# Attention's matmuls in an order written out: projections in steps of twelve, and between them one step of GLA, softmax heads or norms

## The chip, the cores and the metric

The kernel runs on one core of a Trainium2 chip (trn2). The metric is device time in microseconds (us) of one execution. TensorE (PE) multiplies, VectorE (DVE) and ScalarE (ACT) work on tiles and empty PSUM banks, GpSimd (POOL) does a little of that and issues some transfers, SyncE (SP) issues the other transfers. Each engine takes its own instructions strictly in their order.

## The reference

One decoder layer over 512 tokens of width 2048:

```python
xn = rms_norm(h, attn_norm_g)
(gq, gk, gv, gg, ga, fq, fk, fv, fg, ff, mq, mg) = split(xn @ w_in)
log_a = log_sigmoid(ga @ gla_a_w2 + gla_a_b) / 16
gla_o = gla_chunked(heads(gq), heads(gk), heads(gv), heads(log_a))        # 8 heads, dk 64, dv 128
fox_o = forgetting_attention(rms_norm(fq), rms_norm(fk), fv, log_sigmoid(ff + fox_f_b))  # 4 heads of 128, causal
mk, mv = split(rms_norm(mem) @ w_mem_kv)                                  # 256 memory tokens
mem_o = softmax(rms_norm(mq) @ rms_norm(mk).T * 128 ** -0.5) @ mv         # 4 heads of 128
o = rms_norm(concat(gla_o, fox_o, mem_o)) per head
h = x + (o * [silu(gg) | sigmoid(fg) | sigmoid(mg)]) @ w_out
y = h + relu(rms_norm(h, mlp_norm_g) @ w_up) ** 2 @ w_down                # d_ff 8192
```

GLA is a gated linear recurrence: a state per head, decayed by the gates and updated by k^T v. FoX is softmax attention with a cumulative forget term added to the logits.

## The kernel before, in words

All large products are done in three matmuls each: both operands are split into a high part (a cast to a shorter float, on ACT) and a low part (the difference, on DVE), and `mm3` (lines 152 to 156) adds high x high, high x low and low x high. `wtile` (line 136) loads a weight tile through SP's queue and makes both parts; `Weights.split` (line 352) does the same for the blocked products. The stages, in the order of the program:

1. `gk` and `gq` are projected (`project`, line 431), 16 tiles of 128 input columns each.
2. The pairs gv0/gv1 and fq/fk are computed by `in_pair` (line 491) and `multiply` (line 374), with seven block products in place of eight. `ORDER` gives their sequence 1, 5, 6, 3, 7, 2, 4. Four of the seven left operands are sums of blocks of x. `x_sums` (line 447) makes them: the eight tiles of x are read again, ACT multiplies in the gain, POOL makes four sums per tile pair (`block_sums`, line 275, with the engine G), ACT and DVE split them into `sh` and `sl`. This is done before the pairs for the first half of the input columns, and after product 7 of the second pair for the second half. Some differences of weight blocks (`Pair.minus`, line 480) run on POOL too.
3. The constants of attention (masks `tri16`, `suf16`, `cmask`, `lmask`) are made on POOL, lines 523 to 557, in buffers that the pair stage frees.
4. Attention. The 48 columns of gates are projected ("small", line 566). GLA (lines 630 to 742) runs over four chunks of 128 tokens. In each chunk seven levels of block sizes 128 to 2 fill the score matrix: a level takes two differences, an exponential, two products with q into `ql`, one with k, a matmul into `lp`, and a masked copy into `sc`. Then the outputs (line 719) add the state's part (line 715, whose operands have 64 rows) and the state is renewed. Softmax heads go through `attend` (line 402), one head at a time: logits, row maximum, exponential, transposes, product with v. `normed_T` (line 226) and `turned_heads` (line 790) normalise heads and transpose them. Between these stand the projections `fv`, `mq`, the memory's k and v, and the four gates `gg0`, `gg1`, `fg`, `mg`.
5. After each gate projection lines 898 to 918 form the gated heads and the seven left operands of the output product; some go through DRAM (`out_op`).
6. The output product (`out_pair`, line 974), then eight blocks of up and eight of down.

The order of instructions on each engine is set by a planner. It takes them in the order of the program as a priority, moved forward by `high_priority(offset)`, and places what it expects to be ready. `AHEAD` is 3000, `GLA_AHEAD` is 300, `urgent` is 2 x AHEAD. Two pools of four PSUM banks each exist: `gbank` for projections and `abank` for everything else. In the output product the residual block x is loaded by `block` (line 977, priority 300) and added to the product's bank by DVE in `after` (line 988); product 6 goes on in the bank of product 1, so it waits for that addition. Left operands that went through DRAM are read back by `fetch` and split by `resplit` (lines 1051 to 1055, code lines 857 to 868).

Of the kernel before, what the change touches and what calls it, by code (L numbers as in the profile page):

```python
# [15 lines left out]
S = 512  # L16
# [30 lines left out]
def hybrid_layer(  # L47
# [58 lines left out]
    one_c = wide[:, S - 1 : S]  # L106
    fbt = const.tile([FH, 1], F32, name="fbt")
# [5 lines left out]
    def rsqrt(dst, ss, n, inv, name):  # L113

        s, y, z = (const.tile([128, n], F32, name=f"{v}_{name}", tag=f"rs_{v}{n}", bufs=2) for v in "syz")
# [93 lines left out]
    def head_rms(src, nh, name, hd=128):  # L209

        sq = tmp(f"sq_{name}", "tb", nh * hd)
        A.activation(sq, src, AF.Square)
        ss = tp.tile([128, nh], F32, tag="hss", name=f"hss_{name}")
        V.tensor_reduce(ss, sq.rearrange("p (h d) -> p h d", h=nh), AX.X, ALU.add)
        r = tp.tile([128, nh], F32, tag="hr", name=f"hr_{name}", bufs=4)
        rsqrt(r, ss, nh, 1.0 / hd, name)
        return r

    def scaled(dst, ps, rstd, t):
        with tc.high_priority(offset=AHEAD):  # L220
            if t % 2 == 0:
                A.activation(dst, ps, AF.Copy, scale=rstd)  # L222
            else:
                V.tensor_scalar(dst, ps, rstd, None, op0=ALU.mult)

    def normed_T(raw, gain, scale, dst, name):

        r = head_rms(raw, 4, name)
        nrm = tmp(f"nrm_{name}", "tc")
        V.tensor_mul(  # L230
            nrm.rearrange("p (h d) -> p h d", h=4),
            raw.rearrange("p (h d) -> p h d", h=4),
            r.unsqueeze(2).broadcast_to([128, 4, 128]),
        )
        tps = abank(f"tps_{name}")
        for h in range(4):
            T.transpose(tps[:, h * 128 : h * 128 + 128], nrm[:, h * 128 : h * 128 + 128], ident)
        V.tensor_scalar(
            dst, tps.rearrange("p (h t) -> p h t", h=4), gain, scale, op0=ALU.mult, op1=ALU.mult
        )  # L240


    def project(*groups, turned=False, first=False, bank=gbank, order=range(NK // 2)):

        first_k, last_k = 2 * order[0], 2 * order[-1] + 1
        banks = [[(abank if i else bank)(f"{g}_{t}") for t in range(NT)] for i, g in enumerate(groups)]
        for kp in order:
            for ps, group in zip(banks, groups):
                wh, wl = wtile(w_in[GROUPS.index(group), kp], f"{group}{kp}", parts=2 if first and not kp else 1)
                for kk in range(2):  # L250
                    k = 2 * kp + kk
                    ah, al = x_tile(k)
                    for t in range(NT):
                        if turned:
                            cs = slice(kk * 512 + t * 128, kk * 512 + t * 128 + 128)
                            mm3(ps[t], wh[:, cs], wl[:, cs], ah, al, k == first_k, k == last_k)
                        else:
                            cs = slice(kk * 512, kk * 512 + 512)
                            sl = slice(t * 128, t * 128 + 128)
                            mm3(ps[t], ah[:, sl], al[:, sl], wh[:, cs], wl[:, cs], k == first_k, k == last_k)  # L260
        return [p for ps in banks for p in ps]
# [112 lines left out]
    def multiply(w, after, inside=None):  # L374
# [27 lines left out]
    def attend(n, logits, rowmax, v, dst, name):  # L402

        av = abank(f"av_{name}")
# [852 lines left out]
```

## Time and profile before

| what | value |
|---|---|
| median of 3 runs | 2187.0 us (2181.78 to 2187.2) |
| the profiled execution's own time | 2185.21 us |
| its span, first to last instruction | 2183.5 us |
| PE busy | 2126.2 us, 97% |
| DVE busy | 1631.3 us, 75% |
| ACT busy | 1123.2 us, 51% |
| POOL busy | 213.0 us, 10% |
| mean granted clock | 0.993 |

A row of a timeline gives the start in us from the span's start, the length, the engine, the line, the operation, output <- inputs, and the count; the square bracket at the end gives the engine's idle time before it and what ended it. A row of instruction groups gives after the bar the busy time, the mean length of one in ns, and the idle time before. Lengths of matmuls overlap, so the spacing of their starts is the measure of throughput. A short matmul on 32-bit floats is counted as two instructions.

### The profile page before, as it was taken

To read this page: it belongs to the slowest core of one execution; us is meant where nothing else is said; L and a number is where in the kernel's file an instruction comes from. 1 tells how busy PE (TensorE), PEld (TensorE's weight loads), DVE (VectorE), ACT (ScalarE), POOL (GpSimd) and SP (SyncE) were. 2 spreads that over 40 slices of the span, in tenths; PEclk is the share of its full clock that TensorE was granted. 3 is DMA by queue.
4 is the path that set the end of the run, shared out by engine and by line. 5 is a ranking of instruction groups with operands and counts; after the bars stand their busy time and mean duration, and the time that the engine had idled before them with its cause. 6 is when DMAs were issued, how large, how long until landed. Compare 5 with 4: busy or idle time off the path is not lost.

```text
span 2183.5 us, 25488 instructions
## 1 busy us (share of the span) xinstructions
PE 2126.2 (97%) x9746; PEld 1728.5 (79%) x9746; DVE 1631.3 (75%) x1800; ACT 1123.2 (51%) x1535; POOL 213.0 (10%) x245
## 2 busy tenths in 40 slices
PE   8999999989999889999999999999999999999999
PEld 7887777767777668878888888888788788788787
DVE  6579977884666779887768768769868767877875
ACT  6454433344564545755554555556646545556443
POOL 1346100000000003100000000000000000000000
PEclk9999999999999989999999999999999999999999
DMA  7333211241213455533543443455577678668654
GB/s 269 102 118 112 87 59 49 88 143 39 88 61 132 180 217 212 211 117 141 177 144 137 167 168 120 162 182 193 195 219 203 183 202 248 168 191 253 182 167 131
DMA packets 74628, 339.24 MB, mean 155 GB/s; under 512 B 8633, under 2 KB 10681, under 8 KB 53002
## 3 DMA queue, kind: packets, MB, share of 16 engines
q1 hardware_dynamic: 55898, 270.76, 35.3%
q0 software_dynamic: 18608, 66.86, 11.7%
q8 instruction: 76, 1.25, 0.2%
q14 instruction: 46, 0.38, 0.1%
HBM read 266.54 MB, written 71.04 MB: 155 GB/s over the span
## 4 chain that ended last, share of the span: by engine, by line
PE 78%; DVE 11%; DMA 4%; issue 3%; ACT 2%; POOL 1%; SPq 0%; DVEq 0%; ACTq 0%; POOLq 0%
PE acc_up L154 9%; PE acc_up L155 9%; PE acc_up L156 9%; PE acc_dn L155 7%; PE acc_dn L156 7%; PE acc_dn L154 7%; PE acc_out L154 2%; PE acc_out L155 2%; PE acc_out L156 2%; DMA left1l<-op 2%; DVE hl_dn L370 1%; DVE raw_dn L332 1%; DMA left5l<-op 1%; PE gg L154 1%; PE ut L1072 1%
## 5 line engine op out<-in xcount | busy, mean ns | idle before, releaser
L370 DVE TENSOR_TENSOR hl_up<-raw_up,hl_up 128x1024 fp32r<-128x1024 f32 x224 | 271.6, 1221 | 141.6 <-ACT hl_up L370 141.5
L370 ACT CAST hl_up<-raw_up 128x1024 fp32r<-128x1024 f32 x224 | 235.3, 1052 | 253.7 <-PE acc_up L156 193.9
L370 DVE TENSOR_TENSOR hl_dn<-raw_dn,hl_dn 128x1024 fp32r<-128x1024 f32 x224 | 270.5, 1221 | 99.5 <-ACT hl_dn L370 98.7
L370 ACT CAST hl_dn<-raw_dn 128x1024 fp32r<-128x1024 f32 x224 | 234.4, 1053 | 204.6 <-PE acc_dn L156 163.5
L332 DVE TENSOR_TENSOR raw_dn<-raw_dn,raw_dn 128x2048 f32<-128x2048 f32 x64 | 146.1, 2286 | 16.1 <-DMA raw_dn<-in_w_down_dram 15.9
L332 DVE TENSOR_TENSOR raw_up<-raw_up,raw_up 128x2048 f32<-128x2048 f32 x64 | 145.1, 2267 | 1.4 <-DMA raw_up<-in_w_up_dram 1.3
L370 ACT CAST hl_out<-raw_out 128x1024 fp32r<-128x1024 f32 x56 | 58.7, 1052 | 68.6 <-PE acc_out L156 55.3
L1172 POOL DMA_DIRECT2D hd<-m x48 | 41.0, 854 | 516.1 <-ACT m L1171 516.1
L370 DVE TENSOR_TENSOR hl_out<-raw_out,hl_out 128x1024 fp32r<-128x1024 f32 x56 | 69.2, 1253 | 25.0 <-ACT hl_out L370 25.0
L1171 ACT COPY m<-acc_dn 128x512 f32<-128x512 f32 x96 | 54.5, 587 | 30.3 <-PE acc_dn L156 30.3
L1064 POOL DMA_DIRECT2D op<-u x32 | 17.1, 534 | 486.3 <-ACT u L1073 479.1
L370 DVE TENSOR_TENSOR hl_hl_in<-spare,hl_hl_in 128x1024 fp32r<-128x1024 f32 x31 | 45.6, 1481 | 15.6 <-ACT hl_hl_in L370 15.6
L154 PE MATMUL gg<-ahi_x,hl_gg 128*128 128x512 f32 x128 | 54.6, 427 | 2.6 <-ACT raw_mk L222 2.2
L370 ACT CAST hl_hl_in<-spare 128x1024 fp32r<-128x1024 f32 x31 | 32.5, 1049 | 43.4 <-PE acc_in L156 18.9
L155 PE MATMUL acc_dn<-hl_dn,left 128*128 128x512 f32 x128 | 50.3, 393 | 4.6 <-DVE hl_dn L370 4.6
L155 PE MATMUL gg<-alo_x,hl_gg 128*128 128x512 f32 x128 | 53.7, 419 | 0.0
L156 PE MATMUL gg<-ahi_x,hl_gg 128*128 128x512 f32 x128 | 53.2, 415 | 0.0
L154 PE MATMUL acc_up<-hl_up,left 128*128 128x512 f32 x128 | 49.9, 390 | 3.1 <-ACT z L1127 3.1
L155 PE MATMUL acc_in<-hl_hl_in,sh 128*128 128x512 f32 x128 | 50.2, 392 | 2.6 <-DVE hl_hl_in L370 2.6
L155 PE MATMUL acc_dn<-hl_dn,left0h 128*128 128x512 f32 x128 | 50.2, 392 | 1.2 <-DVE hl_dn L370 1.2
L154 PE MATMUL acc_in<-hl_hl_in,sh 128*128 128x512 f32 x128 | 49.9, 390 | 0.7 <-DVE o L499 0.7
L155 PE MATMUL acc_dn<-hl_dn,left3h 128*128 128x512 f32 x128 | 50.5, 395 | 0.0
(566 smaller groups left out, 6320.0 us busy)
## 6 DMA issues: line engine op xcount, KB each, us to landing
raw_up<-in_w_up_dram SPq DMA_DIRECT2D x64, 1024.0 KB, 4.8
raw_dn<-in_w_down_dram SPq DMA_DIRECT2D x64, 1024.0 KB, 6.8
hd<-m POOLq DMA_DIRECT2D x48, 512.0 KB, 5.6
raw_out<-in_w_out_dram SPq DMA_DIRECT2D x16, 1024.0 KB, 5.7
op<-u POOLq DMA_DIRECT2D x32, 512.0 KB, 3.8
op<-s POOLq DMA_DIRECT2D x24, 512.0 KB, 2.9
spare<-in_w_pair_dram SPq DMA_DIRECT2D x16, 512.0 KB, 4.3
raw_in<-in_w_pair_dram SPq DMA_DIRECT2D x16, 512.0 KB, 3.6
```

What stands on the lines that cost most here:

```text
L154: T.matmul(ps, lhsT=ah, rhs=bh, start=start, stop=False, skip_group_check=on)
L155: T.matmul(ps, lhsT=ah, rhs=bl, start=False, stop=False, skip_group_check=on)
L156: T.matmul(ps, lhsT=al, rhs=bh, start=False, stop=stop, skip_group_check=on)
L332: V.tensor_sub(dst, a, b)
L370: made = A.copy(hi, part), V.tensor_sub(lo, part, hi.bitcast(F32))
L1064: nc.gpsimd.dma_start(down_op[c][i][:, half * 1024 : half * 1024 + 1024], tile)
L1072: T.transpose(tps[:, m * 128 : m * 128 + 128], z[:, t * 512 + m * 128 : t * 512 + m * 128 + 128], ident)
L1171: A.copy(st[:, t * 512 : t * 512 + 512], acc[t])
L1172: nc.gpsimd.dma_start(dst, st.rearrange("p (t n) -> p t n", t=2), accum_op=ALU.add)
```

## The change

- **Order.** Attention is rewritten as a generator, `steps`, that runs beside another, `projections`. `projections` hands over after every 12 matmuls (one input tile of a projection). Each `yield n` of attention asks for n such steps before its next burst. Afterwards all PE instructions from "small" to the end of `mg` are chained one behind the other as they were traced, so the planner no longer chooses among them.
- **GLA.** Levels are prepared in pairs one step ahead; the product with k covers only the first half of each block; the state's part uses `qz`, a zero-padded copy of q with 128 rows per head.
- **Softmax.** Heads with short rows share a bank (one, two or four heads), and a three-stage pipeline (`one`: logits, maximum, exponential; `two`: transposes; `three`: product with v) moves one bank per step.
- **Norms.** Sums of squares come from ACT's accumulation, 128 columns at a time, and two blocks share one reciprocal root; transposed results are written by ACT instead of DVE.
- **Operands of the output product.** `place` gives them their buffers only after the memory heads; what the first three gates made by then goes through DRAM and is read back there.
- **Sums of x.** DVE makes them. Those of the second half are made before the pairs, written to DRAM (`x_op`), and read back by operand after products 5, 6, 3 and 7 of the second pair.
- **Output product.** The last gate's banks come from `gbank`, so products 1 and 5 of the first output block swap pools; the x blocks of the first half are loaded with priority 3 x AHEAD.

```diff
             first = p in (1, 5, 2)
             if q == 0 and first:
-                chain[p] = [(gbank if p == 1 else abank)(f"acc_{w.name}_{p}_{i}") for i in range(2)]
+                chain[p] = [(gbank if p == (5 if w.name == "out0" else 1) else abank)(f"acc_{w.name}_{p}_{i}") for i in range(2)]
             acc = chain[p if first else 5 if p == 3 else 1]
...
-    sh = [bp.tile([128, 2, 4, 256], FR, name=f"sh{i}") for i in range(2)]
+    sh = bp.tile([128, 4, 4, 256], FR, name="sh")
...
+    x_op = [dram.tile([128, 4, 256], F32, name=f"x_op{i}") for i in range(4)]
...
-            for _ in block_sums(a1[:, :256], a2[:, :256], a1[:, 256:], a2[:, 256:], temps.get, G):
+            for _ in block_sums(a1[:, :256], a2[:, :256], a1[:, 256:], a2[:, 256:], temps.get):
                 pass
             for i in range(2):
-                hi, lo = (w[j // 2][:, j % 2, 2 * i : 2 * i + 2, :] for w in (sh, sl))
                 src = st[i].rearrange("p (s t) -> p s t", s=2)
-                A.copy(hi, src)
-                V.tensor_sub(lo, src, hi.bitcast(F32))
+                if c:
+                    for s in range(2):
+                        nc.gpsimd.dma_start(x_op[2 * i + s][:, j, :], src[:, s, :])
+                else:
+                    hi, lo = sh[:, 2 * i : 2 * i + 2, j, :], sl[i][:, :, j, :]
+                    A.copy(hi, src)
+                    V.tensor_sub(lo, src, hi.bitcast(F32))
+
+    def next_sums(n):
+        hi, lo = sh[:, n, :, :], sl[n // 2][:, n % 2, :, :]
+        nc.sync.dma_start(lo.bitcast(F32), x_op[n])
+        A.copy(hi, lo.bitcast(F32))
+        V.tensor_sub(lo, lo.bitcast(F32), hi.bitcast(F32))
...
-            if (c, n, p) == (0, 1, 7):
+            if (c, n) == (0, 1) and p in SUMS:
                 with tc.high_priority(offset=AHEAD):
-                    x_sums(1)
+                    next_sums(SUMS[p])
...
     with tc.high_priority(offset=400):
         x_sums(0)
+    x_sums(1)
     for c in range(2):
...
+    def head_rms(srcs, name):
+
+        ss = tp.tile([128, 8], F32, tag="hss", name=f"hss_{name}")
+        for i, src in enumerate(srcs):
+            sq = tmp(f"sq_{name}{i}", "tb")
+            for h in range(4):
+                cs = slice(h * 128, h * 128 + 128)
+                A.activation(sq[:, cs], src[:, cs], AF.Square, accum_out=ss[:, 4 * i + h : 4 * i + h + 1])
+        r = tp.tile([128, 8], F32, tag="hr", name=f"hr_{name}", bufs=4)
+        rsqrt(r, ss, 8, 1.0 / 128, name)
+        return r
...
+    def norms(srcs, gain, dsts, name, wait):
+
+        for a in range(0, len(srcs), 2):
+            r = head_rms(srcs[a : a + 2], f"{name}{a}")
+            nrm = [tmp(f"nrm_{name}{a + i}", "tc") for i in range(2)]
+            for i in range(2):
+                normed(nrm[i], srcs[a + i], r[:, 4 * i : 4 * i + 4])
+            yield wait
+            for i in range(2):
+                tps = abank(f"tps_{name}{a + i}")
+                for h in range(4):
+                    T.transpose(tps[:, h * 128 : h * 128 + 128], nrm[i][:, h * 128 : h * 128 + 128], ident)
+                A.activation(dsts[a + i], tps.rearrange("p (h t) -> p h t", h=4), AF.Copy, scale=gain)
...
+        V.tensor_sub(ev[:, :, :hb], ref, bv[:, :, :hb])
+        V.tensor_sub(ev[:, :, hb:], bv[:, :, hb:], ref)
+        A.activation(e, e, AF.Exp)
+        ql = qls[li % 2]
+        for s in range(2):
+            rows = slice(s * 64, s * 64 + 64)
+            V.tensor_mul(
+                ql[rows, :, s, :].rearrange("p h (n b) -> p h n b", b=hb),
+                qTs[rows, c, :].rearrange("p (h n b) -> p h n b", h=4, b=B)[:, :, :, hb:],
+                e[rows, :].rearrange("p (h n b) -> p h n b", h=4, b=B)[:, :, :, hb:],
+            )
+
+        V.tensor_mul(ev[:, :, :hb], ev[:, :, :hb], blocks_of(kTs[:, c, :], B)[:, :, :hb])
+        return li, e, ql
...
+    def gla(g):
+        state = tmp("state", "rbx")
+        bT, eb, kd = decays(0, g)
         for c in range(NT):
-            if c == 2:
-                for t in range(NT):
-                    normed_T(o[:, t, 1536:2048], g_fk, 1.0, fkT[:, :, t * 128 : t * 128 + 128], f"fk{t}")
-            qT, kT = qTs[:, c, :], kTs[:, c, :]
-
...
+
+            qk = tmp(f"qk_{c}", "tc")
+            G.tensor_tensor(qk, qTs[:, c, :], kTs[:, c, :], op=ALU.mult)
+            ready = [level(c, li, bT) for li in (0, 1)]
+            yield 2 if c else 3
+            for a in (0, 2, 4, 6):
+                lps = [(li, level_scores(c, li, e, ql)) for li, e, ql in ready]
+                if a == 4 and c < NT - 1:
+                    g = decay_logs(c + 1)
+                if a == 6:
+                    dps = abank(f"dg_{c}")
+                    for p in range(4):
+                        T.matmul(
+                            dps[:, 2 * p : 2 * p + 2], lhsT=qk[:, p * 128 : p * 128 + 128], rhs=sel,
+                            start=True, stop=True,
+                        )
+                    dg = tp.tile([128, GH], F32, tag="dg", name=f"dg_{c}")
+                    V.tensor_copy(dg, dps[:, :GH])
+                for li, lp in lps:
+                    place_scores(li, lp)
+                ready = [level(c, li, bT) for li in (a + 2, a + 3) if li < len(LEVELS)]
+                if a == 4 and c:
+                    for s in range(2):
+                        rows = slice(s * 64, s * 64 + 64)
+                        V.tensor_mul(qz[rows, :, s, :], heads4(qTs[:, c, :])[rows], heads4(eb)[rows])
+                yield 3 if a in (0, 4) else 2
...
+                    T.matmul(dst, lhsT=qz[:, p, s, :], rhs=state[:, p * 128 : p * 128 + 128], start=True, stop=False)
...
+            if c < NT - 1:
+                yield 1
+                bT, eb, kd = decays(c + 1, g)
+            if c == 0:
+                yield from norms([o[:, t, 1536:2048] for t in range(NT)], g_fk, tokens(fkT), "fk", 1)
...
+    def softmax_heads(parts):
+        banks = [Bank(a, h0) for a in parts for h0 in range(0, 4, 4 // a.n)]
+        for i in range(len(banks) + 2):
+            if i >= 2:
+                banks[i - 2].three()
+            if 1 <= i <= len(banks):
+                banks[i - 1].two()
+            if i < len(banks):
+                banks[i].one()
+            yield 1
...
+        mrstd = token_rstd(macc, MT, "mem")
+        mks = room.rearrange("p (m c) -> p m c", m=MT)
+        for m in range(MT):
+            V.tensor_scalar(mks[:, m, :], mks[:, m, :], mrstd[:, m : m + 1], None, op0=ALU.mult)
+            A.activation(mv[:, m, :], mraw[:, m, :], AF.Copy, scale=mrstd[:, m : m + 1])
+        dsts = [mkT[:, :, m * 128 : m * 128 + 128] for m in range(MT)]
+        yield from norms([mks[:, m, :] for m in range(MT)], g_mk, dsts, "mk", 2)
+        yield 1
+        yield from norms([o[:, t, 1536:2048] for t in range(NT)], gains[:, 1:2], tokens(mqT), "mq", 2)
...
+    def steps():
+        g = yield from first_steps()
+        yield 2
+        yield from gla(g)
+        assert mem_ready
+        yield 1
+        late["rbg"] = tmp("rbg", "rbx")
+        tp.tile([128, 40], F32, tag="fill", name="fill_tp", bufs=1)
+        spread(spread_dg(xrstd, "g"), late["rbg"], "g")
+        for n in range(2):
+            yield from turned_heads(n, 2)
+        yield from softmax_heads([Fox(t) for t in reversed(range(NT))])
+        yield from memory_norms()
+        yield from turned_heads(2, 2)
+        yield from softmax_heads([Mem(t) for t in range(NT)])
+        place()
+        yield from turned_heads(3, 2)
...
+    def project_steps(group, turned=False, order=range(NK // 2)):
+
+        first_k, last_k = 2 * order[0], 2 * order[-1] + 1
+        ps = [gbank(f"{group}_{t}") for t in range(NT)]
+        for kp in order:
+            wh, wl = wtile(w_in[GROUPS.index(group), kp], f"{group}{kp}")
+            for kk in range(2):
+                k = 2 * kp + kk
+                for t in range(NT):
+                    if turned:
+                        cs = slice(kk * 512 + t * 128, kk * 512 + t * 128 + 128)
+                        mm3(ps[t], wh[:, cs], wl[:, cs], xh[k], xl[k], k == first_k, k == last_k)
+                    else:
+                        cs = slice(kk * 512, kk * 512 + 512)
+                        sl = slice(t * 128, t * 128 + 128)
+                        mm3(ps[t], xh[k][:, sl], xl[k][:, sl], wh[:, cs], wl[:, cs], k == first_k, k == last_k)
+                if k != last_k:
+                    yield
+        return ps
 
...
+            early = i in (A11, S1) or i == S2 and not last
+            if early and high:
                 hi, lo = halves(high[i][:, cs]), halves(lower(i, cs))
                 A.copy(hi, src)
                 V.tensor_sub(lo, src, hi.bitcast(F32))
             else:
                 nc.gpsimd.dma_start(halves(out_op[i][:, cs]), src)
+                if early:
+                    waiting.append((i, cs))
...
+    def place():
+
+        high.update({A11: bigt(2, [128, 2048], f"left{A11}h", FR), S1: bigt(3, [128, 2048], f"left{S1}h", FR)})
+        low.update({A11: [bigt(0, [128, 2048], f"left{A11}l", FR)], S1: [bigt(1, [128, 2048], f"left{S1}l", FR)]})
+        left2 = third.tile([128, 2048 + CUT], FR, tag="third", name=f"left{S2}")
+        high[S2], low[S2] = left2[:, :2048], [left2[:, 2048:]]
+        for i, cs in waiting:
+            fetch(i, cs, out_op[i][:, cs])
+            resplit(i, cs)
...
+    def projections():
+        ps = yield from project_steps("fv")
+        for t in range(NT):
+            A.activation(o[:, t, 1024:1536], ps[t], AF.Copy, scale=rs_x(t))
+        yield
+        ps = yield from project_steps("mq")
+        for t in range(NT):
+            A.activation(o[:, t, 1536:2048], ps[t], AF.Copy, scale=rs_x(t))
+        yield
...
+    last_banks = []
+    attention = steps()
+    wait = next(attention)
+    for _ in projections():
+        wait -= 1
+        if wait <= 0:
+            wait = next(attention, 1 << 20)
+    assert 3 in heads_of
+    traced = nc.cur_bb.bb.instructions
+    first = next(i for i in reversed(range(len(traced))) if traced[i] is mark) + 1
+    on_pe = [i for i in traced[first:] if i.engine == T.engine]
+    for a, b in zip(on_pe, on_pe[1:]):
+        tc.add_manual_dep(
+            b, a.name, mybir.DependencyInfo(mybir.DependencyClass.NoSync, mybir.DependencyReason.DATA), reason="order"
+        )
...
 
         def block(r, c):
 
-            with tc.high_priority(offset=300):
+            with tc.high_priority(offset=300 if n else 3 * AHEAD):
                 z[r, c] = stage(f"x_{n}_{r}{c}")
                 nc.sync.dma_start(z[r, c].rearrange("p (t n) -> p t n", t=2), x[r, 2 * n + c])
```

More of the change, by code (lines that the diff above doesn't have):

```diff
@@ L207, in token_rstd, with project @@
         return r
[L209 to L247, printed above, removed]
+    def project(*groups):
+        banks = [[(abank if i else gbank)(f"{g}_{t}") for t in range(NT)] for i, g in enumerate(groups)]
+        for kp in range(NK // 2):
             for ps, group in zip(banks, groups):
-                wh, wl = wtile(w_in[GROUPS.index(group), kp], f"{group}{kp}", parts=2 if first and not kp else 1)
+                wh, wl = wtile(w_in[GROUPS.index(group), kp], f"{group}{kp}", parts=1 if kp else 2)
                 for kk in range(2):
@@ L621, in hybrid_layer @@
+    spread(dgs, rbx, "x")
     sc = op2.tile([128, GH, 128], F32, name="scores")
@@ L870, in halves @@
[L870 to L897 removed]
+        heads_of[n] = ot
```

562 lines of the change are left out of this document (287 added, 275 removed).

## The prediction

> **What bounds the kernel now.** I read the times by stretch first: they show where TensorE (PE) has slack. Columns: microseconds, then busy time and count of PE, PE's weight loads, DVE, ACT and POOL, then granted clock, DMA share, GB/s.
>
> ```profile
> span 2183.5 us, 25488 instructions
> ```
> ```profile
> 95.70:254.00 158.30, 154.27 (x674) 125.61 (x674) 132.88 (x123) 73.60 (x88) 66.39 (x47) 1.00 0.32 107
> 254.00:731.40 477.40, 464.97 (x2315) 358.73 (x2314) 329.61 (x724) 215.67 (x422) 16.89 (x19) 0.99 0.25 84
> 759.60:774.30 14.70, 0.20 (x1) 0.00 (x0) 14.70 (x13) 9.53 (x10) 0.00 (x0) 0.62 0.96 383
> ```
> ```profile
> 700.00:731.25 31.25, 31.25 (x140) 25.85 (x139) 13.25 (x15) 8.67 (x10) 0.56 (x1) 1.00 0.48 170
> ```
>
> The stages are the block products of the input pairs, attention (the "small" product to the last gate projection), and a hole 28 us into the output product. PE bounds all but that third row, where it stands still and DVE works throughout. "Busy" hides slack, because matmuls overlap; a 512-column matmul in an undisturbed stretch costs 31.25/138 = 0.2267 us (the two cut by the edges left out). So the pair stage needs 672 x 0.2267 = 152.3 us and takes 158.3. Attention has 1392 such matmuls (1344 of projections, 48 "small"), 315.6 us; the other 161.8 are its own short matmuls and losses.
>
> Second, PE's waits in attention and in the output product's start (total, times, longest):
>
> ```profile
> PE lp L686 <- DVE e L683: 4.1, 12, 0.6
> PE tps_mq L237 <- DVE nrm_mq L230: 3.0, 2, 2.0
> PE gg L154 <- ACT raw_mk L222: 2.2, 1, 2.2
> PE mg L154 <- ACT o L801: 1.5, 1, 1.5
> PE fg L154 <- DVE z_gg L901: 0.8, 1, 0.8
> PE gg L154 <- DVE z_gg L901: 0.4, 1, 0.4
> ```
> ```profile
> PE acc_out L154 <- DVE x L988: 14.5, 1, 14.5
> ```
>
> That is 12.0 us in eighteen small waits, and one of 14.5, the largest in the kernel.
>
> **Part 1, the pair stage.** The sums of x leave POOL for DVE, both halves are made before the pairs, and the second half goes through DRAM. In POOL's timeline of before:
>
> ```profile
> 166.30 1.71 POOL L280 TENSOR_TENSOR st<-xs 128x256 f32<-128x256 f32 x1
> 171.59 0.20 POOL L524 MEMSET tri<- 128x128 f32 x1 [3.58 <-issue]
> ...
> 189.23 5.29 POOL L481 TENSOR_TENSOR spare<-raw_in,spare 128x1024 f32<-128x1024 f32 x2
> ```
>
> The masks (tri to lmask, 171.6 to 189.2, 17 us) start when the second half's sums end, whose buffers they take over, and stand ahead of weight differences (L481) whose splits PE needs. With early sums the masks should come early too. Price: 32 adds on DVE at 0.42 (L672 below, 128x256 with two inputs) = 13.5 us, on 132.9 of 158.3: it fits, though tightly. The 16 small writes and four reads of 512 KB go beside a DMA share of 0.32; each read is asked for about seven products (7 x 24 x 0.2267 = 38 us) before its use, which is its cover; uncovered, each would stall PE by a landing. At most 158.3 - 152.3 = 6.0 can be won; if DVE's 13.5 fall half on the path, 7 are lost. I take **-3** (-6 to +7).
>
> **Part 2, attention, what goes.** (a) The state product now has 128 rows (a zero-padded qz) instead of 64. Without a state product, then with it:
>
> ```profile
> 321.67 1.95 PE L719 MATMUL o<-o,scores 128*128 128x128 f32 x16
> 323.55 1.09 PE L724 MATMUL st<-o,kd 128*64 128x128 f32 x16
> ```
> ```profile
> 466.98 0.39 PE L154 MATMUL mkv<-hl_mem,memh 128*128 128x512 f32 x1
> 467.30 0.48 PE L715 MATMUL o<-state,qe 64*128 64x128 f32 x2
> ```
> ```profile
> 473.54 0.49 PE L719 MATMUL o<-o,scores 128*128 128x128 f32 x2
> 473.79 0.47 PE L155 MATMUL mkv<-hl_mem,memh 128*128 128x512 f32 x1
> 474.10 0.39 PE L156 MATMUL mkv<-hl_mem,meml 128*128 128x512 f32 x1
> ```
>
> 16 instructions in 1.88 us are 0.118 each; 32 in 6.49 are 0.203. Over three chunks, 96 x 0.085 = 8.2 us.
>
> (b) Fewer changes between projection and attention. Above, entering takes 0.32 instead of 0.227 (466.98 to 467.30), leaving 0.31 (473.79 to 474.10): 0.18 per burst. The timeline of before holds 121 bursts from 265.12 (spread_x) to 684.27 (ot). The new code's steps make about 62: 3 at first, 26 in GLA (per chunk one for decays, four for pairs of levels, one for the outputs, partly run together, and two for fk), 3 for spread and turned heads, 13 Fox, 5 memory norms, 12 to the end. 59 x 0.18 = 10.6 us.
>
> (c) The waits of before, 12.0 us, and the clock they cost:
>
> ```profile
> 489.41 0.80 PE L154 MATMUL gg<-ahi_x,hl_gg 128*128 128x512 f32 x1 [2.23 <-ACT raw_mk L222]
> 490.00 0.63 PE L155 MATMUL gg<-alo_x,hl_gg 128*128 128x512 f32 x1
> 490.43 0.63 PE L156 MATMUL gg<-ahi_x,hl_gg 128*128 128x512 f32 x1
> ```
>
> After the 3.0 us for nrm_mq and 2.2 for raw_mk, all within 7 us, matmuls come every 0.43 us; eleven of them lose 2.4. Without all this attention would take 477.4 - 12.0 - 2.4 - 8.2 - 10.6 = 444.2.
>
> **Part 3, attention, what comes.** PE's order is now fixed: a burst that isn't ready stops everything behind it, projections too. Between bursts lie 1 to 3 steps of 12 matmuls, 2.72 us each. In GLA DVE must keep up (rows of GLA and memory; 128x512 multiplies L683 become half as wide):
>
> ```profile
> L690 DVE COPY_PREDICATED scores<-lmask,lp 128x512 f32<-128x512 int32 x28 | 24.9, 889 | 2.9 <-PE lp L686 2.8
> L678 DVE TENSOR_TENSOR ql<-qTs,e 64x256 f32<-64x256 f32 x56 | 24.4, 435 | 0.6
> L147 DVE TENSOR_TENSOR hl_mem<-raw_mem,hl_mem 128x1024 fp32r<-128x1024 f32 x16 | 19.5, 1218 | 0.9 <-ACT hl_mem L146 0.8
> L673 DVE TENSOR_TENSOR e<-bT 128x256 f32<-128x256 f32 x28 | 12.3, 438 | 0.3
> L672 DVE TENSOR_TENSOR e<-bT 128x256 f32<-128x256 f32 x28 | 11.8, 421 | 4.6 <-ACT bT L651 4.4
> L739 DVE SCALAR_TENSOR_TENSOR o<-o,dg,o 128x128 f32<-128x128 f32 x32 | 9.0, 342 | 12.0 <-PE st L724 9.0 <-PE o L719 2.8
> L165 DVE SCALAR_TENSOR_TENSOR meml<-spare,colt,memh 128x256 fp32r<-128x256 f32 x14 | 6.7, 482 | 1.6 <-ACT memh L164 1.3
> ```
>
> One level costs 0.889 + 0.421 + 0.438 + 2 x 0.435 + 0.42 = 3.04 us of DVE, seven 21.3; with L739 (2.7), the state's update and qz (4 in all, an estimate from those rows) a chunk has 28. Its 13 steps give 35.4 us of projections and some 14 of bursts; weight splits add 1.22 every second step. That fits outside the memory product. There each step brings 1.218 + 0.482 + 0.421 = 2.12 (splits of weights and memory, and the squares' add, 128x256 with two inputs as in L672): 16 x 2.12 + 28 x 16/13 = 68.4 us of DVE against 16 x 2.72 + 14 x 16/13 = 60.8 of PE. So 7.6 wait. At the starts of three chunks L739 stands before the new levels: 2 us each, 6. At six changes of projection the first bank must be emptied (0.7, a DVE or ACT instruction of 512): 4. Together 18, my value; bounds 5 (the order fits as well as before) and 65 (2.5 us at each of 26 GLA bursts). Norms move from DVE reductions to sums on ACT:
>
> ```profile
> L412 ACT ACTIVATE p_f<-ls,nmx_f 128x128 f32<-128x128 f32 x4 | 1.6, 402 | 3.1 <-DVE nmx_f L824 3.1
> L412 ACT ACTIVATION_READ_ACCUMULATOR p_f<-ls,nmx_f 128x1 f32 x16 | 3.0, 188 | 0.0
> ```
>
> 120 of them (30 blocks of four heads) at 0.402 + 0.188 are 71 us, for 30 squares over 512 columns before. ACT is busy 216 of 477, so the steps hide this; with the cover gone, one norm pair late by its eight sums would hold a burst for 4.7, which lies inside the bound of 65. Operands of the first three head groups take a way through DRAM and are read back after the memory heads; some eleven steps (30 us) of the last projection hide that, and uncovered it would delay the output product's first operand by one landing. Attention: 444.2 + 18 = 462, **-15**.
>
> The Trainium skill (TensorE: Matmul & The Clock Gate, Part 1: The HAM clock gate) lets PE fall to half clock only after an idle window of about 3.4 us. The trace differs: waits of 1.0, 2.0 and 2.2 sufficed. By that page, waits under 2.5 us would cost nothing more; by the row, 5.2 us of them close together cost 2.4. I charge none to the 18, as they lie apart, but add it to the slower rival.
>
> **Part 4, the output product's start.** Its x blocks for the first half get a priority of 3 x AHEAD instead of 300.
>
> ```profile
> 760.05 1.06 SPq L864 DMA_DIRECT2D left2l<-oo  x2
> 762.76 3.54 SPq L981 DMA_DIRECT2D x<-in_x_dram  x3
> ```
> ```profile
> 771.32 2.35 DVE L859 TENSOR_TENSOR left1l<-left1l,left1h 128x1536 fp32r<-128x1536 f32 x2
> 773.59 1.28 DVE L988 TENSOR_TENSOR x<-x,acc_out 128x512 f32<-128x512 f32 x2
> ```
>
> Now x is loaded behind the operands, and its add stands behind their splits on DVE, while product 6 waits for the bank. Loaded early, the add runs at once and product 6 may start at 759.6: 14.7 us, and 1.4 of slow clock after it. Late next are the splits for product 6 and operands 4 to 6: DVE is busy in all of 759.6 to 774.3 and that work stays. I give back 4: **-12** (-16 to 0; zero if x's tile comes free late or the add keeps its place). On SP the x loads pass weight loads of product 5, some 1 us, within the 4.
>
> **Sum.** The profiled execution took 2185.21 us (span 2183.5), 1.8 under the median of 2187.0, within its runs. 2185.2 - 3 - 15 - 12 = **2155**.
>
> **Rivals.** R1, waits twice as long: the score copies stand before the next levels on DVE, so a two-step gap (5.44) ends late by 2.5 us in two pairs of each chunk, 20 more: 2175. For it: DVE's row of 329.6 busy. Against: PE waited 4.1 for these tiles before. R2, slower: the fixed order waits 2.5 us at every GLA burst, 65 instead of 18: 2202, and with the clock falling, 65/5.2 x 2.4 = 30 more, 2232. It decides once waits pass 477.4 - 444.2 + 15 = 48, or 1.8 us at each of 26 bursts. Against: only the memory steps overfill DVE. R3: the early x changes nothing at 759.6, the add still behind DVE's queue: 2167.
>
> **Chances.** Forecast 0.54, R1 0.18, R3 0.15, R2 0.13. This kernel's measurement tells about 0.3% from no change, 6.6 us. The forecast lies below 2180, R3 all but 0.01, R1 0.13 of 0.18; R2 holds slower 0.11 and same 0.02. Faster 0.81, same 0.08, slower 0.11. The range 2130 to 2184 leaves out 0.06 below (waits of 5, everything else won) and 0.13 above.
>
> **What would show it.** Right: attention near 462 us with some 62 bursts, no instruction with 64 rows, PE's waits near 18 and most of them in the memory product; the wait of acc_out for x gone; pair stage near 155. Wrong: waits for e, ql or bT over 40 us, a clock under 0.95 in GLA, or a hole of over 8 us after product 5.

## The result and the profile after

The changed kernel takes 2210.5 us (median; 2207.6 to 2212.2), the kernel before 2186.1 on the same chip: a ratio of 1.0114, 95% interval [1.0096, 1.0132]. It is slower by 1.1%, where 2155 (2130 to 2184) was forecast. The profiled execution:

```profile
span 2210.5 us, 25633 instructions
```

By stretch, in the columns that the prediction explains: the pair stage, attention and the output product, then three parts of attention behind GLA, and last the same output product before the change.

```profile
96.10:252.80 156.70, 153.79 (x675) 125.81 (x675) 136.58 (x121) 72.26 (x83) 53.17 (x40) 1.00 0.37 120
252.70:764.70 512.00, 466.75 (x2316) 376.76 (x2314) 301.15 (x605) 236.51 (x606) 21.51 (x28) 0.94 0.27 87
764.70:935.70 171.00, 162.89 (x729) 133.81 (x728) 152.22 (x136) 104.70 (x153) 33.77 (x39) 0.98 0.66 240
...
516.00:550.00 34.00, 21.01 (x85) 15.72 (x84) 22.74 (x55) 25.63 (x97) 1.07 (x2) 0.75 0.12 39
616.00:660.00 44.00, 33.36 (x147) 27.22 (x146) 30.52 (x69) 33.30 (x123) 4.37 (x7) 0.84 0.31 103
704.00:735.00 31.00, 21.84 (x79) 17.08 (x78) 19.28 (x37) 19.14 (x48) 4.38 (x7) 0.78 0.43 136
```
```profile
731.40:913.30 181.90, 163.21 (x729) 133.97 (x729) 151.95 (x136) 105.16 (x153) 33.80 (x39) 0.94 0.61 225
```

The pair stage went from 158.3 to 156.7 us (-1.6), the output product from 181.9 to 171.0 (-10.9), and attention from 477.4 to 512.0 (**+34.6**). The up and down products, whose code is the same, take 1274.8 us instead of 1270.2 in this execution (in that of a_gate below 1269.8). So attention is where the change loses, and PE's granted clock fell there from 0.99 to 0.94. The same view of waits as in the prediction, over attention after the change:

```profile
PE ot L944 <- DVE o L590: 10.4, 3, 4.6
PE gg L156 <- DVE z_gg L1014: 6.6, 1, 6.6
PE lp L737 <- DVE e L731: 5.6, 2, 4.6
PE tps_mk L603 <- DVE nrm_mk L590: 5.0, 1, 5.0
PE tps_mq L603 <- DVE nrm_mq L590: 5.0, 1, 5.0
PE mg L156 <- DVE z_fg L1014: 4.5, 2, 3.6
PE lf L656 <- DVE lfT L575: 3.6, 1, 3.6
PE pT_f L898 <- ACT p_f L890: 1.9, 1, 1.9
PE mkv L156 <- ACT o L1053: 0.8, 2, 0.6
PE fg L156 <- DVE z_gg L1014: 0.6, 1, 0.6
PE lg_f L830 <- ACT o L946: 0.5, 1, 0.5
PE lg_m L861 <- ACT o L946: 0.5, 1, 0.5
PE mkv L157 <- DVE hl_mem L149: 0.2, 1, 0.2
```

Together 45.2 us against 12.0 before. Read it by place: lf, lp and mkv are the start of attention and GLA with its projections, 10.2 us. All else, 35.0 us, is behind GLA: transposes of turned heads (ot), the memory norms (tps_mk, tps_mq), and projections (gg, mg, fg) that need a PSUM bank which a gate has not emptied yet (z_gg, z_fg).

What PE waited for at 522 to 542 begins on ACT. Its timeline there:

```profile
519.75 0.31 ACT L584 ACTIVATE sq_on<-o 128x128 f32<-128x128 f32 x1 [5.93 <-PE spread_g L566]
519.97 0.18 ACT L584 ACTIVATION_READ_ACCUMULATOR sq_on<-o 128x1 f32 x1
520.06 0.29 ACT L584 ACTIVATE sq_on<-o 128x128 f32<-128x128 f32 x1
...
522.44 0.21 ACT L119 ACTIVATE y_on<-s_on 128x8 f32<-128x8 f32 x1
...
522.85 1.03 ACT L148 CAST hl_gg<-raw_gg 128x1024 fp32r<-128x1024 f32 x1
523.78 0.20 ACT L120 ACTIVATE y_on<-y_on 128x8 f32<-128x8 f32 x1
...
531.04 0.61 ACT L572 ACTIVATE ee_gg<-z_gg 128x512 f32<-128x512 f32 x1
```

And PE's over the same time (an instruction's wait stands in brackets):

```profile
522.28 0.39 PE L158 MATMUL gg<-ahi_x,hl_gg 128*128 128x512 f32 x1
526.69 0.98 PE L944 MATMUL ot<-ident,o 128*128 128x128 f32 x2 [4.02 <-DVE o L590]
529.45 3.64 PE L944 MATMUL ot<-ident,o 128*128 128x128 f32 x14 [1.77 <-DVE o L590]
532.73 0.78 PE L156 MATMUL gg<-ahi_x,hl_gg 128*128 128x512 f32 x1
...
534.59 0.63 PE L157 MATMUL gg<-alo_x,hl_gg 128*128 128x512 f32 x1
535.01 0.63 PE L158 MATMUL gg<-ahi_x,hl_gg 128*128 128x512 f32 x1
542.20 0.80 PE L156 MATMUL gg<-ahi_x,hl_gg 128*128 128x512 f32 x1 [6.56 <-DVE z_gg L1014]
```

DVE reads the gate's banks (z_gg):

```profile
520.77 1.29 DVE L1014 TENSOR_TENSOR z_gg<-gg,rbg 128x512 f32<-128x512 f32 x2
...
541.46 1.28 DVE L1014 TENSOR_TENSOR z_gg<-gg,rbg 128x512 f32<-128x512 f32 x2
```

In the code the squares' scratch tile shares its two buffers with spread_g's diagonal tiles, so no square starts before spread_g's matmuls, which ACT's first row names as its releaser. From 519.75 the squares stand nearly back to back on ACT, those of the next head group with them. From the first square to the first transpose (526.69) 6.9 us pass: eight squares, and then the short steps of the reciprocal root on ACT and DVE, with the cast of a weight (522.85) and squares of the next pair between them. PE has one projection step to do meanwhile, 12 matmuls or 2.7 us. The code asks for two steps there, but when the projection gg0 ends, the gate that follows calls for its turned heads at once (`while n not in heads_of: next(attention)`). So PE, whose order is fixed, stands at the first transpose for 4.0 us and 1.8 more behind it.

The gate's first function on ACT (ee_gg) comes only at 531.04, behind the squares. As z_gg has two scratch tiles, DVE empties the third and fourth bank only when ACT and DVE have done with the first two, at 541.46. Until then PE gets half a projection step done (6 matmuls, for two banks) and stands for 6.6. ACT is busy 25.6 of these 34 us, 33.3 of 44 at 616 to 660, and 19.1 of 31 at 704 to 735. Matmuls that came every 0.227 us start every 0.42 between the waits (534.59 to 535.01).

### The profile page after: what moved, and what is told of

It is laid out like the page before. It is cut to its first block, busy times and chain, and to the rows that moved or that the text cites. A ratio compares the mean times of both kernels' runs of the same rounds, so it can differ in the third digit from the quotient of the medians.

```text
span 2210.5 us, 25633 instructions
## 1 busy us (share of the span) xinstructions
PE 2130.1 (96%) x9746; PEld 1747.9 (79%) x9746; DVE 1617.7 (73%) x1711; ACT 1142.7 (52%) x1715; POOL 195.5 (9%) x239
## 4 chain that ended last, share of the span: by engine, by line
PE 79%; DVE 10%; DMA 4%; ACT 3%; issue 3%; SPq 0%; DVEq 0%; ACTq 0%
PE acc_up L156 9%; PE acc_up L158 9%; PE acc_up L157 9%; PE acc_dn L157 7%; PE acc_dn L158 7%; PE acc_dn L156 7%; PE acc_out L157 2%; PE acc_out L156 2%; PE acc_out L158 2%; DMA left1l<-op 2%; DVE hl_hl_in L333 2%; DVE hl_dn L333 1%; PE gg L156 1%; DVE raw_dn L295 1%; PE gg L158 1%
## 5 line engine op out<-in xcount | busy, mean ns | idle before, releaser
L157 PE MATMUL acc_in<-hl_hl_in,sh 128*128 128x512 f32 x128 | 50.4, 394 | 2.9 <-DVE hl_hl_in L333 2.9
L157 PE MATMUL acc_dn<-hl_dn,left3h 128*128 128x512 f32 x128 | 50.8, 397 | 0.0
L156 PE MATMUL acc_dn<-hl_dn,left3h 128*128 128x512 f32 x128 | 50.7, 396 | 0.0
L156 PE MATMUL acc_up<-hl_up,left0h 128*128 128x512 f32 x128 | 50.5, 394 | 0.0
## 6 DMA issues: line engine op xcount, KB each, us to landing
hd<-m POOLq DMA_DIRECT2D x48, 512.0 KB, 5.4
op<-u POOLq DMA_DIRECT2D x32, 512.0 KB, 3.5
op<-s POOLq DMA_DIRECT2D x24, 512.0 KB, 3.3
spare<-in_w_pair_dram SPq DMA_DIRECT2D x16, 512.0 KB, 4.1
raw_in<-in_w_pair_dram SPq DMA_DIRECT2D x16, 512.0 KB, 4.2
```

The lines of the kernel that those rows point to most:

```text
L156: T.matmul(ps, lhsT=ah, rhs=bh, start=start, stop=False, skip_group_check=on)
L157: T.matmul(ps, lhsT=ah, rhs=bl, start=False, stop=False, skip_group_check=on)
```

## The experiments

The theories' names are those of the texts written before each run. Each ratio is to the kernel before on the same chip, with its 95% interval. The last columns are of attention in the profiled execution (us): its length, PE's waits, the time at half granted clock, and PE's changes from projections to other work.

| kernel | time | ratio | attention | waits | half clock | bursts |
|---|---|---|---|---|---|---|
| before | 2186.1 | 1 | 477.4 | 12.0 | 6.8 | 121 |
| changed | 2210.5 | 1.0114 [1.0096, 1.0132] | 512.0 | 45.2 | 61.4 | 60 |
| a_free: no chain of PE's order | 2163.6 | 0.9902 [0.9887, 0.9917] | 467.0 | 11.7 | 20.5 | 84 |
| a_oldnorm: norm sums on DVE | 2208.5 | 1.0108 [1.0093, 1.0123] | 510.4 | 44.1 | 51.2 | 60 |
| a_wait: longer gaps at norms | 2190.1 | 1.0027 [1.0018, 1.0035] | 492.3 | 33.6 | 37.5 | 60 |
| a_gla: chain to GLA's end only | 2176.5 | 0.9966 [0.9952, 0.9979] | 477.6 | 20.0 | 23.9 | 77 |
| a_tail: chain behind GLA only | 2193.5 | 1.0042 [1.0027, 1.0058] | 497.3 | 36.7 | 44.4 | 67 |
| a_gate: gates ahead | 2211.8 | 1.0130 [1.0113, 1.0148] | 515.2 | 51.8 | 64.9 | 60 |
| a_wait_gate: both | 2187.2 | 1.0008 [0.9999, 1.0018] | 487.9 | 30.9 | 34.1 | 60 |
| a_free_gate: no chain, gates ahead | 2149.6 | 0.9836 [0.9817, 0.9855] | 455.6 | 6.1 | 3.4 | 90 |
| b_x: before + early x | 2174.2 | 0.9960 [0.9946, 0.9974] | 478.0 | 12.0 | 10.2 | 121 |
| b_qz: before + 128-row product | 2181.0 | 0.9986 [0.9978, 0.9995] | 471.9 | 13.2 | 10.2 | 120 |
| b_three: before + x, qz, sums of x | 2170.3 | 0.9936 [0.9922, 0.9950] | 471.8 | 12.8 | 10.2 | 120 |
| b_three_gate: that + gates ahead | 2172.0 | 0.9952 [0.9935, 0.9968] | 474.7 | 13.8 | 13.7 | 120 |

**The chain taken away (a_free).** All else of the change stays; only the planner again chooses among ready matmuls.

```diff
-    for a, b in zip(on_pe, on_pe[1:]):
+    for a, b in ():
```

> The changed kernel, but its PE instructions are not chained: the planner orders them again, with all other parts kept. Theory O (the fixed order itself costs the 34 us that attention lost): the planner fills the holes with projection matmuls, PE's waits in attention fall from 45 us to under 20 and the clock stays up; attention goes to about 465, the whole to 2160 to 2175. Theory N (the norm and gate chains are late whatever order PE has): the waits stay over 35 us and the whole stays at 2200 or more.

Measured: 2163.6 us, 47 less than with the chain (46 by the ratios), and 20 less than before the change: theory O. Its waits in attention:

```profile
PE ot L944 <- DVE o L590: 5.3, 6, 2.9
...
PE tps_mk L603 <- DVE nrm_mk L590: 0.3, 1, 0.3
```

The norms' waits have gone (tps_mk 0.3, no tps_mq): while a burst isn't ready, PE does projections. The fixed order alone turns a gain of 20 us into a loss of 24.

**The form of the norms' sums (a_oldnorm).** One square over 512 columns on ACT and the sum on DVE, as before the change, with the chain kept.

```diff
-            for h in range(4):
-                cs = slice(h * 128, h * 128 + 128)
-                A.activation(sq[:, cs], src[:, cs], AF.Square, accum_out=ss[:, 4 * i + h : 4 * i + h + 1])
+            A.activation(sq, src, AF.Square)
+            V.tensor_reduce(ss[:, 4 * i : 4 * i + 4], heads4(sq), AX.X, ALU.add)
```

> The changed kernel with the order kept, but a block's sum of squares is taken as before: one square over 512 columns on ACT and one reduction on DVE, in place of four sums of 128 columns on ACT. Theory N (the form of the sums makes the chain too long: 16 sums of 0.295 us stand in ACT's queue per head group): the waits for turned heads, mk, mq and the gates fall from 31 us to under 12, and with the clock's share the whole comes to 2175 to 2190. Theory G (two steps are too few for the chain in either form): it moves by less than 8 us, and DVE's reductions take the place of ACT's sums in front of the waits.

Measured: 2208.5, with an interval that overlaps the changed kernel's: theory G. The waits for turned heads, mk, mq and the gates are 27.9 us instead of 32.1. Who makes the sums isn't the cause; what stands between them and their transposes on PE is the same.

**Longer gaps (a_wait).** The numbers of projection steps between the squares and the transposes.

```diff
-        yield from norms([mks[:, m, :] for m in range(MT)], g_mk, dsts, "mk", 2)
+        yield from norms([mks[:, m, :] for m in range(MT)], g_mk, dsts, "mk", 4)
...
-            yield from turned_heads(n, 2)
+            yield from turned_heads(n, 3 if n else 4)
```
The steps of mq and of the last two turned_heads go from 2 to 3 as well.

> The changed kernel with nine more steps between a norm and the burst that needs it (turned heads 4, 3, 3, 3 instead of 2 each; mk 4, mq 3 instead of 2). Theory G: each of these bursts finds its operands ready or nearly; waits for turned heads, mk and mq fall from 20 us to under 6, the clock drops to half fewer times, and the whole comes to 2180 to 2190; the waits for the gates' banks (12 us) stay. Theory O would see the waits move to the next bursts and the whole stay over 2200.

Measured: 2190.1, 20 less, about what theory G says. The norms' waits fell from 10.0 to 1.2 and those of ot from 10.4 to 5.8, but the gates' banks stayed:

```profile
PE gg L156 <- DVE z_gg L1014: 7.8, 1, 7.8
PE ot L944 <- DVE o L590: 5.8, 2, 4.0
PE fg L156 <- DVE z_gg L1014: 5.5, 1, 5.5
```

The 5.8 left at ot are both of the first head group, and the edit didn't reach them: there the gate still calls for the heads after one step (spread_g at 518.96, 12 matmuls, then the transposes at 526.77). Where the gap did grow, 13.4 of 14.6 us went. So too short a gap is a cause of part of the loss, and a bank that a gate holds is another, which a longer gap does not touch.

**Where the chain costs (a_gla, a_tail).** The chain kept on one part only (in a_tail the part is on_pe[cut:]).

```diff
         yield from gla(g)
+        ends.append(nc.cur_bb.bb.instructions[-1])
...
+    end = next(i for i in reversed(range(len(traced))) if traced[i] is ends[0])
+    cut = sum(i.engine == T.engine for i in traced[first : end + 1])
+    part = on_pe[:cut]
+    for a, b in zip(part, part[1:]):
```

> The changed kernel with its chain cut after GLA: PE's instructions are held in the written order up to the last of GLA, and the planner orders the rest. Free throughout it took 2164, chained throughout 2210. If the fixed order costs where PE's waits stood (10 us of waits and 17 us of half clock in GLA and its start, 35 us and 44 us behind it), this one keeps about a quarter of the loss: 2172 to 2180. If the forecast was right that GLA is the dear place, 2190 or more.

> The changed kernel with the chain only behind GLA (turned heads, softmax heads, norms, gates). By the place of the waits it keeps about three quarters of the loss: 2190 to 2202. If GLA were the dear place, 2175 or less. The two losses over 2164 should add up to about 46.

Measured against a_free: 13 us for GLA's part, 30 for the part behind it, 43 of the 47, as the waits' places had said. GLA, which the prediction went through step by step, carries the smaller share.

**The parts alone, on the kernel before (b_x, b_qz, b_three).** The priority of the x blocks; the zero-padded qz; both with the sums of x.

```diff
-            with tc.high_priority(offset=300):
+            with tc.high_priority(offset=300 if n else 3 * AHEAD):
```
```diff
+    qz = spare[:, 6 * M : 10 * M].rearrange("p (h s t) -> p h s t", h=4, s=2)
+    G.memset(qz, 0.0)
...
-                        dst, lhsT=qe[s : s + 64, p * 128 : p * 128 + 128],
-                        rhs=state[s : s + 64, p * 128 : p * 128 + 128], start=True, stop=False,
+                        dst, lhsT=qz[:, p, h % 2, :], rhs=state[:, p * 128 : p * 128 + 128], start=True, stop=False,
```

> The kernel before with one number changed: the x blocks of the output product's first half are loaded with priority 3 x AHEAD. If the early load alone removes the hole before product 6, the output product's start shortens by 10 to 13 us and the whole comes to 2174 to 2177. If the changed kernel's hole shrank for another reason (the swapped pools, other operands already in place), it stays within 4 us of before.

> The kernel before with the state's product over 128 rows (zero-padded q) and nothing else. By the spacing of the rows (0.203 against 0.118 us, 96 instructions) it wins 8.2 us: 2174 to 2178. Against that, two half-row products replace one on DVE, and where GLA is held by DVE the gain is hidden: then 2180 to 2184.

> The kernel before with the three parts that lie outside attention's rewriting or need none of it: early x blocks, the 128-row state product, the sums of x made early on DVE and re-read by operand. If the parts add up (9.5 measured, 8.2 and 2 worked out): 2162 to 2167, as good as the rewritten attention without its chain. If the planner shifts other waits into the place, 2170 or more.

Early x alone: the output product takes 170.2 us instead of 181.9, the times' ratio says 0.4%, as expected. Its waits for x:

```profile
PE acc_out L154 <- DVE x L988: 2.6, 1, 2.6
```

The qz alone shortens attention by 5.5 us and the time by 0.14%, some 3 us: less than the 8.2 worked out, and outside its first range. Waits grew by 1.2, and the half clock cost 1.6 more (10.2 us with 2.2 of waiting in them, against 6.8 with 2.1), so the product itself won about 8.3. The half clock grew in b_x too, where attention is as before. All three give 0.64%, some 14 us, about what b_x, b_qz and the pair stage's 1.1 add up to. The rest of the change without the chain (attention's traced order, and its new forms of GLA, softmax and norms, which no run took apart) is worth some 7 us more than these (a_free against b_three).

**The gates ahead (a_gate, a_wait_gate, a_free_gate, b_three_gate).** What is traced for a gate gets a higher priority on ACT and DVE; PE has no part in it.

```diff
-            gate(n, ps)
+            with tc.high_priority(offset=AHEAD):
+                gate(n, ps)
```

> The changed kernel with one edit: all that is traced for a gate (its products with the banks, its sigmoid, its block sums) gets a priority of AHEAD, so that ACT and DVE take it ahead of the squares of the next head group or of the norms, which are traced before it. PE's order is as in the changed kernel. Theory Q (the gates' banks are emptied late because ACT first does up to 36 squares that nobody needs yet): the waits of gg, fg and mg for z_gg and z_fg (11.7 us with those of before the softmax) fall under 4, and the time to about 2198. Rival S (the gate only takes the place of the squares; then the turned heads and the norms come later by as much): those waits go, but those of ot, tps_mk and tps_mq (20.4 us) grow by 5 or more, and the time stays within 2207 to 2215.

> The changed kernel with both edits: three or four projection steps between the squares of turned heads or norms and their transposes, and the gates' work at a priority of AHEAD. The longer gaps alone gave 2190.1, with 13.3 us of waits for z_gg left. Theory Q: these go too, 13 us and their half clock: 2172 to 2178. Rival S: the longer gaps are needed by the squares that the gates now push back, so ot, mk and mq wait again: 2186 to 2195.

> The changed kernel without the chain of PE's order, and the gates' work at a priority of AHEAD. Without the chain alone the time was 2163.6, with waits of 11.7 us, of which 4.2 for z_gg and 5.3 at the turned heads. Theory Q: 2158 to 2162, the waits for z_gg under 1. Rival S: what the gate wins the turned heads lose, 2162 to 2166.

> The kernel before with the early x, the 128-row state product and the sums of x re-read by operand (together 2170.3 us, attention 471.8), and the first three gates' work at a priority of AHEAD. If the gates' late order is worth 14 us in any free order of PE, as it was in the changed kernel without its chain (2163.6 to 2149.6), this gives 2154 to 2160. If that gain rests on the rewritten traced order of attention, the waits of this kernel's attention (12.8 us, of them 1.2 for z_gg) leave little to win: 2167 to 2172, and some 20 us of what the version without chain gains belong to the rewritten order.

With the chain the rival S holds. The wait of gg is gone, but the first rows of a_gate's waits are now

```profile
PE ot L944 <- DVE o L590: 20.4, 6, 9.0
PE tps_mk L603 <- DVE nrm_mk L590: 18.6, 1, 18.6
```

The gate takes ACT and DVE first, the squares come later, and PE stands at the transposes instead: 2211.8, as slow as the changed kernel. With longer gaps too, the waits are 30.9 instead of 33.6 and the time is 2187.2: S again, the fixed order only gets to the time of the kernel before. Without the chain the same edit was expected to give at most 6 us, and gave **14**: 2149.6 us, 0.9836 [0.9817, 0.9855] of the time before, the best kernel here. Attention there, where the largest wait is one of 4.4 for turned heads:

```profile
252.40:708.00 455.60, 449.05 (x2315) 359.38 (x2314) 299.83 (x605) 235.74 (x606) 21.54 (x28) 1.00 0.30 98
```

The waits fell by 5.6 us, and the time at half clock from 20.5 to 3.4; neither theory had counted that. In b_three_gate the edit won nothing (2172.0 against 2170.3, the ratios' intervals overlap): those 14 us need the rewritten attention.

## Why the prediction was wrong, point by point

**Part 1** (-3): the pair stage took 1.6 us less. Right within its bounds. (31.25/138 is 0.2264, not 0.2267; over attention's 1392 matmuls that is 0.4 us, and no term of the sum hangs on it.)

**Part 2, what goes**: right. (a) In the profile after, the state product (L788) and the score product (L789) alternate, all with 128 rows:

```profile
512.57 0.38 PE L788 MATMUL o<-state,spare 128*128 128x128 f32 x2
512.79 0.39 PE L789 MATMUL o<-o,scores 128*128 128x128 f32 x2
...
515.91 0.39 PE L789 MATMUL o<-o,scores 128*128 128x128 f32 x2
```

30 instructions in 3.34 us are 0.111 each instead of 0.203; the prediction had 0.118. (b_qz, which has this alone, bears out the 8.2, less what its waits and clock took back.) (b) 60 bursts, where about 62 were counted. The base of 444.2 us can be tested on a_free_gate: 455.6 less its waits of 6.1 is 449.5; its 90 bursts instead of 62 cost, at the prediction's 0.18, 5.0 more than the base: 449.2.

**Part 3, what comes**: this is the step that failed, in two of its terms. The first is "Together 18, my value". The waits were 45.2. The memory product's 7.6 came about as priced: both waits for lp (5.6) and one of 0.2 for a split lie in it. Of the 6 at the starts of chunks there is 1.1 at most (one of the lp waits), and 3.6 at lf, ahead of GLA, had no price. "At six changes of projection the first bank must be emptied (0.7 [...]): 4" measured 11.7 at the three changes behind a gate and 0.8 at mkv: emptying took as long as the chain that frees the two scratch tiles, which began behind the squares on ACT, and not the 0.7 of one instruction. And for turned heads and norms, priced at nothing, it measured 20.4. The price at hand for one late pair ("late by its eight sums would hold a burst for 4.7") is near the 5.0 met at mk and at mq, but by luck: eight sums take 2.4 us, and the chain's other steps and the work between them make up the rest. What hid them was to be "ACT is busy 216 of 477": an average over attention. In the stretches in which the waits fall ACT was busy for 0.62 to 0.76 of the time (19.1 of 31, 25.6 of 34, 33.3 of 44), and its queue held the sums of a later head group and a gate at once.

The estimate of the sums' work was even too high; their groups in attention after the change:

```profile
L584 ACT ACTIVATE sq_on<-o 128x128 f32<-128x128 f32 x64 | 18.8, 295 | 6.0 <-PE spread_g L566 5.9
L584 ACT ACTIVATION_READ_ACCUMULATOR sq_on<-o 128x1 f32 x64 | 12.0, 187 | 0.0
```

and in the timeline above a square and its read come every 0.29 to 0.31 us, not every 0.59. So the load was not the error. A fixed order asks for one tile at one moment, and what answers is the chain that makes the tile, with all that stands in the queues between its steps, against the PE work left in front of it (6.9 against 2.7 us at the first head group); the maker's share of busy time doesn't tell.

The second term is "I charge none to the 18, as they lie apart" of the clock. 444.2 + 45.2 = 489.4, and attention took 512.0: the 22.6 left go to the clock, by subtraction. The trace agrees: of 61.4 us at half clock PE waited for 16.7, and the other 44.7, in which matmuls start at 0.42 instead of 0.227, cost half of it, 22.4. By the trace's record of the granted clock they came in eight stretches, six of 6.83 us and two of 10.24, and each began within, or less than 1 us after, a gap of 3.97 to 7.18 us between two starts on PE. Gaps up to 2.3 us that stood alone started none here, nor did one of 2.65 in a_wait; in the kernel before, 1.4, 2.2 and 2.5 within 7.3 us did. The Trainium skill (TensorE: Matmul & The Clock Gate, Part 1: The HAM clock gate) has an idle window of about 3.4 us after which the clock halves; the changed kernel's single waits agree with it, and stretches of 6.83 and 10.24 are near two and three such windows. Not all runs agree: a gap of 2.90 that stood alone was followed by 3.41 us at half clock (b_three_gate, at 681), and one of 3.68 by none (a_gla, at 618). The prediction set the page aside for a row of short waits close together, and did not ask what the page says of one wait of 4 us.

**Part 4** (-12): -10.9 in the stage, and -11.7 with that edit alone, where the wait for x fell from 14.5 to 2.6. Right.

**The rivals.** R2 had the sign and nearly its point (it "decides once waits pass" 48: 45.2, and the clock); its times were 2202, and 2232 with the clock falling, and 2210.5 lies between. But it put the waits at GLA's 26 bursts, and "Against: only the memory steps overfill DVE" answered for GLA alone. The signs of "right" did fail: waits near 18, most of them in the memory product, where 6.6 of 45.2 were found. Those of "wrong" (waits for e, ql or bT over 40 us, a clock under 0.95 in GLA, a hole after product 5) did not occur either: 35 us of the waits lie behind GLA, for which they named nothing. R1 put 20 us more at GLA's pairs of levels, where lp waited 5.6 in all, and R3 fell with Part 4.

**What stays open.** That the squares wait for spread_g through a shared scratch buffer is read from one row and the code; a version with a buffer of their own was not run. Neither was one with more scratch tiles for z_gg, with a longer gap at the first head group, or with gaps that fit the queues as they then are, so this does not show that no fixed order could win.

## What to carry to other kernels

Pinning an in-order engine's order turns each late tile into a stall of everything behind it: before pinning, go through every point where it would wait, add up the chain that makes the tile and what stands in the queues between its steps, and hold that against the work left in front of the point; the maker's average load is no answer. Look up in the trace whether the gaps asked for are the gaps that came. Free matmuls that can fill in (projections here) are worth more unpinned: the same change with the traced order only as the planner's preference was 20 us faster than the kernel before, and 35 once the work that empties banks had priority. Price a single wait of 4 us or more on PE with the slow clock after it: here 45 us of waits cost some 23 more.

## What the runs showed of the hardware that wasn't expected

A 128x128 sum of squares on ACT, with the read of its sum, starts every 0.29 us in a row: the read (0.187) overlaps the squares around it. The prediction's 0.402 + 0.188 were the rows of an exponential, and added what overlaps: in the kernel before its read starts 0.31 us after it. And the granted clock's slow stretches after a single wait were not in proportion to it. Except where the span ends, all of them, in all fourteen profiles, last a multiple of 3.41 us. Gaps of 3.97 and 7.18 us both came with 6.83; the same gap of 3.97 at the start of attention was followed by 6.83 here, in a_wait and in a_gate, but by 3.41 in a_gla and a_wait_gate. A gap of 4.41 with one of 2.25 behind it came with 10.24 here and with 6.83 in a_wait, and in a_free_gate one of 4.80 with only 3.41.
